# An instruction planner with other costs, gathered rows' readers placed later, and sums of squares on TensorE

## The chip, the cores and the metric

The kernel runs on one core of a Trainium2 chip. The metric is device time in microseconds (us) of one execution. The core has five engines that run their own instruction streams in order: PE (TensorE; its weight loads are listed as PEld), DVE (VectorE), ACT (ScalarE), POOL (GpSimd) and SP (SyncE, which here only starts DMA transfers).

## The reference, cut to what matters

One inference step of a two-layer decoder: 512 prompt tokens and 8 sample tokens (one new token for each of 8 sequences) with shared weights. Layer A is a Mamba-2 mixer (chunked scan, 4 groups, chunks of 128 tokens), layer B attention in three dilation groups against a shared K/V (for the sample rows: gathered from caches). Caches are also returned, shifted by one row.

```python
def mamba2_mixer(u, conv_prev, ssm_prev, w_in, conv_w, conv_b, dt_bias, a_log, d_skip, norm_w, w_out):
    z, xbc, dt = jnp.split(u @ w_in, [D_INNER, D_INNER + CONV_DIM], axis=-1)
    xbc, conv_new = causal_dwconv(xbc, conv_prev, conv_w, conv_b)
    ...
    y, ssm_new = ssd_scan(xs, dt, a, bm, cm, ssm_prev)      # h_t = exp(a*dt_t) h_{t-1} + dt_t x_t B_t^T, y_t = C_t h_t
    y = y + xs * d_skip[:, None]
    h = y * jax.nn.silu(z)
    hg = h.reshape(h.shape[:-1] + (SSM_GROUPS, D_INNER // SSM_GROUPS))
    hg = hg * lax.rsqrt(jnp.mean(hg * hg, -1, keepdims=True) + RMS_EPS)      # the sums of squares
    return (hg.reshape(h.shape) * norm_w) @ w_out, conv_new, ssm_new

def dilated_group_sample(q, k_all, v_all, buf_len, window, dil, slopes):     # 16 heads, 3 dilation groups
    steps = jnp.arange(window // dil + 1)
    idx = buf_len + jnp.arange(n_new)[:, None] - steps[None, :] * dil
    kg, vg = k_all[:, idx_c], v_all[:, idx_c]                                # gathered keys and values
    scores = jnp.einsum('bthd,btkhd->bthk', q, kg) * ATT_SCALE + bias
    ...
hp = layer_norm(DEEPNORM_ALPHA * hp + dp, ln_g[layer], ln_b[layer])          # after each layer
```

## The kernel before, in words

**A planner writes the order.** The kernel is built by Python generators on a clock of their own (class Order). Each generator issues instructions through an Eng object, which adds an estimated duration (Eng.cost) to that engine's planned time, and then sleeps until the planned end plus LAT (300 ns) before it issues what depends on it. What is emitted is one fixed instruction stream for each engine, in planned order; on the chip an engine takes its stream strictly in that order, and waits at the first instruction whose inputs are not there. A transfer's planned end comes from class Dma: a rate of 355 GB/s, some fixed delays, one queue. A Flag holds a tile's planned time; wait(flag) sleeps until then; take and give hand out the buffers of a pool; calm(engine) sleeps until the engine's planned queue is nearly empty; tt picks DVE or POOL, whichever is planned to end first. All instructions go through one helper line (157), so the profile's groups differ by tile names and not by lines; DMA issues have line 206.

**Layer A.** For each of four groups g the weights of x, B, C (6 tiles of 128 output columns) and later of the gate z (4 tiles) are loaded (`wst`), split into a rounded part and a rest (`whi` by ACT, `wlo` by DVE), and multiplied with the split input (tiles `xh`, `xl`): 48 matmuls a tile. The order is x0, x1, z0, x2, z1, x3, z2, z3. When the six x tiles of a group are planned, ssd(g) starts: for each chunk c of four, decay (M, CE from rows `Abc` read back by DMA), stage1 (CBm, xdt, xde), states (hst), stage2 (by, yt, the gate, and the sum of squares for the group's norm in v[:, 0, c]), and once a group sample(): eight sequences' states `hs` are loaded, multiplied with B and C rows (`bcb`), updated and stored. sample_end normalises the sample rows, and the group's own norm follows (tile hreg). Then the out projection out_unit runs over the groups (half 0: groups 0 to 3 with the split tiles hh, hl and for samples hsm; then half 1), the layer norm, and the split of its result (x1h, x1l).

**Layer B.** For each head pair hp of eight, ten projections (three K, V, Q and a gate; 48 matmuls each) alternate with attn(hp) for the prompt (scores from KT and QT tiles in 64 rows, P, then PT) and sample(hp) for the 8 samples. sample(hp) writes its query rows to DRAM (q_scr) and reads them back spread over all partitions: six loads `qb` through three buffers (qload). kgather loads three tiles `kg` of gathered keys a head pair, through two buffers. On DVE (or POOL) each half of a kg tile is multiplied with its qb and summed (tile sc); the scores then go through the softmax to the matmuls with `vg`. evac moves each projection out of PSUM: DVE writes the 8 sample columns (tile sT), ACT the rest (KT, QT, vT), and K and V tiles are transposed on PE. Between all of this the copier issues 168 pieces of the cache copy from ACT's queue. At the end the out projection of layer B and the layer norm run.

The lines the text speaks of: the costs in Eng.cost; stage2's sum of squares; one(), the per-sequence part of ssd's sample(); ssd's loop over chunks; kgather and qload. Their planned times of arrival are set so:

```python
f_kg[hp, g].t = end + LAT                       # kgather
f.t = dma(SP, qb, ...) + LAT                    # qload
yield from wait(fq); yield from calm(V, G)      # sample(hp)
end = tt(kt[:, bs], kt[:, bs], fq.tile, OP.mult)
```

Of the kernel before, what the change touches and what calls it, by code (L numbers as in the profile page):

```python
# [10 lines left out]
F32 = mybir.dt.float32  # L11
# [3 lines left out]
OP = mybir.AluOpType  # L15
AX = mybir.AxisListType

P = 128
# [16 lines left out]
RS = 2.0 ** -13  # L35
SLOPES = [2.0 ** (-8.0 * (h + 1) / 16) for h in range(16)]
LAT = 300.0
DMA_RATE = 355.0
ACT_ISSUE = 200.0
SMALL = 110.0  # L40
# [16 lines left out]
class Order:  # L57
# [8 lines left out]
    def spawn(self, gen, prio=1):  # L66
        self.seq += 1
        heapq.heappush(self.heap, (self.now, prio, self.seq, gen))
# [12 lines left out]
    def wait(self, *flags):  # L81
        for f in flags:
            while f.t is None:
                yield self.now + 100.0
            if f.t > self.now:
                yield f.t
# [41 lines left out]
class Eng:  # L128
    def __init__(self, order, raw, kind, port=None):
        self.o, self.raw, self.kind, self.free, self.port = order, raw, kind, 0.0, port  # L130

    def spend(self, cost, shared=False):
        t = max(self.free, self.o.now)
# [26 lines left out]
    def cost(self, name, a, k):  # L160
        if self.kind == "PE":
            mv = k["rhs"] if name == "matmul" else a[0]
            n = _n(mv)
            if name == "transpose":
                return 112.0
            if mv.dtype == F32:
                m = a[0].shape[0]
                return max(214.0, 4 * n / 2.4 + 4) * (0.35 if m == 32 else 0.63 if m == 64 else 1.0)
            return max(57.0, n / 2.4 + 13)
        if self.kind == "V":  # L170
            src = a[1]
            n = max(_n(a[0]), _n(src))
            if name in ("tensor_copy", "tensor_scalar") and not _psum(src):
                n /= 2
            if name == "reciprocal":
                n *= 6
            return (66 + n) / 0.96 + (SMALL if n < 64 else 15.0)
        if self.kind == "S":
            p = sum(1 for v in ("bias", "scale") if hasattr(k.get(v), "shape")) + (1 if "accum_out" in k else 0)
            return (112 + _n(a[0])) / 1.2 + 93 * p + 10  # L180
        n = _n(a[0])
        if name == "tensor_scalar":
            return 90 + 1.2 * n
        if name == "partition_broadcast":
            return 200 + 1.15 * n
        return 90 + (2.08 if name == "tensor_tensor" else 1.4) * n
# [27 lines left out]
def yoco_step(  # L214
# [17 lines left out]
    def dram(ap, off, dims):  # L232
        return bass.AP(tensor=ap.tensor, offset=ap.offset + off, ap=[list(d) for d in dims])
# [41 lines left out]
    def tt(out, a, b, op, slack=-100.0):  # L275

        n = _n(out)
        two = _sbuf(a) and _sbuf(b)
        ev = max(V.free, od.now, port.free if two else 0.0) + (66 + n) / 0.96
        eg = max(G.free, od.now, port.free) + 90 + 2.08 * n  # L280
        e = V if ev <= eg - slack else G
        e.tensor_tensor(out, a, b, op)
        return e.free
# [147 lines left out]
    def calm(*engines):  # L431

        while True:
            t = min(e.free for e in engines) - CALM
            if t <= od.now:
                return
            yield t
# [258 lines left out]

    f_hk = {(g, k): Flag() for g in range(GROUPS) for k in range(4)}
    f_hn = [Flag() for _ in range(GROUPS)]
    f_p = [Flag() for _ in range(GROUPS)]
    f_old = {(g, b): Flag() for g in range(GROUPS) for b in range(NS)}  # L700

# [10 lines left out]
    def ssd(g):  # L712
# [14 lines left out]
        def sample():  # L727
# [29 lines left out]
            def one(b, hs, end, bc):  # L757
                yield end + LAT
                tmp = yield from take(pN, [P, 4, P], "tmp", 2)
                yield from calm(V)  # L760
                for i in range(4):
                    V.tensor_tensor_reduce(tmp[:, i, :], hs[:, i, :], bc[:, 1, b % 2, :], 1.0, 0.0, OP.mult, OP.add, ys[:, i, b:b + 1])
                done[0] += 1
                if done[0] == NS:
                    f_s.t = V.free + LAT
                yield V.free + LAT
                yield from calm(S)
                for i in range(4):
                    S.activation(tmp[:, i, :], bc[:, 0, b % 2, :], AF.Copy, scale=xdts[:, i, b:b + 1])
                left[b // 2] += 1  # L770
                if left[b // 2] == 2:
                    give(pN, "bcb", S.free)
                yield S.free + LAT
                yield from calm(V)
                for i in range(4):
                    V.scalar_tensor_tensor(hs[:, i, :], hs[:, i, :], selv[:, 4 * g + i, b:b + 1], tmp[:, i, :], OP.mult, OP.add)
                give(pN, "tmp", V.free)
                yield V.free + LAT
                yield from dma.ready()
                give(pN, "hs", dma(S, dram(ssm_s, (b * DI + g * 512) * P, [[P, P], [P * P, 4], [1, P]]), hs))  # L780
                last[0] += 1
                if last[0] == NS:
                    give(pN, "xdts", S.free)
# [99 lines left out]
        def stage2(c):  # L883
# [32 lines left out]
            sq = yield from take(pS, [P, 4, P], "sq", 2)  # L916
            S.activation(sq, hv, AF.Square)
            yield S.free + LAT
            yield tt(sq[:, 0:2], sq[:, 0:2], sq[:, 2:4], OP.add, SLACK2) + LAT
            yield tt(sq[:, 0], sq[:, 0], sq[:, 1], OP.add, SLACK2) + LAT  # L920
            b = yield from bank()
            PE.matmul(b[:, 0:1], lhsT=sq[:, 0, :], rhs=ones[:, 0:1], start=True, stop=True)
            give(pS, "sq", PE.free)
            yield PE.free + LAT
            V.tensor_scalar(v[:, 0, c:c + 1], b[:, 0:1], 512.0 * EPS, None, OP.add)
            unbank(V.free)
            f_q[c].t = V.free

        def sample_end():
            yield from wait(f_s, f_sx, *[f_z[g, i] for i in range(4)])  # L930
# [28 lines left out]
            V.tensor_tensor(hv, hv, nw[:, 4 * g:4 * g + 4].unsqueeze(2).to_broadcast([P, 4, NS]), OP.mult)  # L959
            f_hn[g].t = V.free + LAT  # L960

        for c in range(4):
            for hg in range(2):
                spawn(decay(c, hg))
            spawn(stage1(c))
            spawn(states(c))
            spawn(stage2(c))
            if c == 0:
                spawn(sample())
            yield from wait(f_1[c])  # L970
        yield from wait(f_st[3])
        b = yield from bank()
# [376 lines left out]
    def layer_b(XB, pL, early):  # L1349
# [69 lines left out]
        def kgather():  # L1419
            for hp in range(8):  # L1420
                for g, (c, L, dil) in enumerate(caches):
                    kt = yield from take(pQ, [P, NS, P], "kg", 2)
                    end = dma(SP, kt, dram(c, hp * P, [[dil * ROW, P], [L * ROW, NS], [1, P]]))
                    f_kg[hp, g].tile = kt
                    f_kg[hp, g].t = end + LAT

        def vgather():
            for hp in range(8):
# [244 lines left out]
        def qload(hp, ready):  # L1673

            yield ready
            for g in range(3):
                for hb in range(2):
                    qb = yield from take(pB, [P, 4, P], "qb", 3)
                    f = f_qb[hp, g, hb]
                    f.tile = qb  # L1680
                    f.t = dma(SP, qb, dram(q_scr[hp], (g * NS + 4 * hb) * P, [[0, P], [P, 4], [1, P]])) + LAT
                    yield od.now

        def sample(hp):
# [256 lines left out]
```

## Time and profile before

| | us |
|---|---|
| median of 3 runs | 1242.2 |
| lowest and highest of them | 1235.66 and 1245.82 |
| the profiled execution | 1242.98 |
| its span, first to last instruction | 1241.2 |

The median is what a change is compared with. The profiled execution is the one that the trace shows; 1.8 us of it lie outside its span. Times in the rows below are us from the start of the span. An arrow in square brackets names the idle time of the engine just before an instruction and what ended it.

### The profile page before, as it was taken

Reading aid. Unit: us, or ns where it says so; the run is one execution under the profiler, and the core shown is the slowest. Engines: PE = TensorE matmul, PEld = TensorE weight load, DVE = VectorE, ACT = ScalarE, POOL = GpSimd, SP = SyncE. Lnnn points to the kernel's source line nnn. Section 1 sums busy time; section 2 is a strip of 40 time slices with the busy share of each in tenths; the row PEclk is TensorE's granted clock in tenths of the full one; section 3 lists DMA queues with packets and bytes.
Section 4 is the critical chain, followed back from the end, with each engine's and each line's share of the span. In section 5 each row is a group of like instructions: output and inputs, shape, how many; then the busy total and the mean of one; then the engine's idle time right before and its main releaser. Section 6 shows DMA issues by size and latency. Waiting matters only on the chain.

```text
span 1241.2 us, 23709 instructions
## 1 busy us (share of the span) xinstructions
PE 1124.5 (91%) x9114; PEld 1025.5 (83%) x9114; DVE 810.5 (65%) x2458; ACT 562.2 (45%) x1295; POOL 78.2 (6%) x152
## 2 busy tenths in 40 slices
PE   7999879989999799897999997989999999899994
PEld 6898869879886566897899897978989989899763
DVE  3989799799799647534727536346256373482878
ACT  3467766666666322343344442433334334333432
POOL 0011011020011001000001000010001000100000
PEclk9999979989999999899899998998999999999997
DMA  9889989898987888998899997998999989964421
GB/s 293 292 264 295 315 254 321 260 312 289 319 309 263 305 302 259 315 312 276 267 322 311 317 347 234 345 289 258 311 305 344 313 289 328 326 184 142 143 107 69
DMA packets 259466, 344.56 MB, mean 278 GB/s; under 512 B 10513, under 2 KB 240633, under 8 KB 256629
## 3 DMA queue, kind: packets, MB, share of 16 engines
q10 hardware_dynamic: 45068, 197.51, 44.4%
q1 hardware_dynamic: 214286, 145.55, 41.1%
q8 instruction: 71, 1.16, 0.4%
q14 instruction: 41, 0.34, 0.1%
HBM read 319.36 MB, written 199.82 MB: 418 GB/s over the span
## 4 chain that ended last, share of the span: by engine, by line
PE 45%; DMA 24%; DVE 22%; ACT 4%; issue 3%; SPq 1%; ACTq 0%; POOL 0%; DVEq 0%; POOLq 0%
PE ps L157 45%; DMA qb<-q_scr 5%; DVE wlo L157 3%; DMA bcb<-bc_scr 3%; DVE rt L157 3%; DMA wst<-in_a_in_proj_dram 2%; DMA wst<-in_kv_proj_dram 2%; DVE hreg L157 2%; DMA kg<-in_cache_kv_w_dram 2%; DMA out_dram<-hs 2%; DMA q_scr<-sq 2%; DMA Abc<-a_scr 2%; DVE xs L157 1%; ACT whi L157 1%; DVE al L157 1%
## 5 line engine op out<-in xcount | busy, mean ns | idle before, releaser
L157 PE MATMUL ps<-x1h,whi 128*128 128x256 f32 (+1 forms) x1280 | 281.8, 299 | 11.3 <-DVE G L157 11.3
L157 PE MATMUL ps<-x1l,whi 128*128 128x256 f32 (+1 forms) x1280 | 266.8, 287 | 0.0
L157 PE MATMUL ps<-x1h,wlo 128*128 128x256 f32 (+1 forms) x1280 | 266.7, 287 | 0.0
L157 ACT CAST whi<-wst 128x1024 fp32r<-128x1024 f32 x145 | 150.4, 1041 | 206.9 <-PE ps L157 177.8
L157 DVE TENSOR_TENSOR wlo<-wst,whi 128x1024 fp32r<-128x1024 f32 x143 | 174.3, 1222 | 96.2 <-ACT whi L157 88.0
L157 PEld LDWEIGHTS ps<-x1h,whi 128*128 128x128 f32 x1280 | 205.4, 195 | 18.8 <-DVE G L157 11.7
L157 PEld LDWEIGHTS ps<-x1l,whi 128*128 128x128 f32 x1280 | 205.7, 193 | 0.0
L157 PEld LDWEIGHTS ps<-x1h,wlo 128*128 128x128 f32 x1280 | 205.4, 193 | 0.0
L157 PE MATMUL ps<-xh,whi 128*128 128x256 f32 (+3 forms) x656 | 145.5, 299 | 3.4 <-DVE hreg L157 2.9
L157 PE MATMUL ps<-xl,whi 128*128 128x256 f32 (+3 forms) x656 | 135.4, 284 | 0.0
L157 PE MATMUL ps<-xh,wlo 128*128 128x256 f32 (+3 forms) x656 | 135.3, 284 | 0.0
L157 DVE TENSOR_SCALAR sT<-ps 128x8 f32<-128x8 f32 x72 | 11.8, 164 | 170.0 <-PE ps L157 169.9
L157 PEld LDWEIGHTS ps<-xh,whi 128*128 128x128 f32 (+1 forms) x656 | 103.3, 189 | 11.3 <-issue 6.1
L157 PEld LDWEIGHTS ps<-xl,whi 128*128 128x128 f32 (+1 forms) x656 | 102.9, 188 | 0.2
L157 PEld LDWEIGHTS ps<-xh,wlo 128*128 128x128 f32 (+1 forms) x656 | 102.6, 187 | 0.2
L157 ACT ACTIVATE P<-P,nm 128x256 f32<-128x256 f32 (+1 forms) x128 | 61.8, 486 | 51.1 <-DMA out_dram<-sq 12.6
L157 ACT COPY PT<-ps 128x512 f32<-128x512 f32 (+1 forms) x64 | 33.1, 564 | 61.0 <-PE ps L157 59.8
L157 DVE CUSTOM_DVE_ANT_0 P<-ps,bias 128x256 f32<-128x256 f32 (+1 forms) x128 | 46.7, 402 | 9.6 <-PE ps L157 8.6
L157 ACT ACTIVATE M<-Abc,ncs 128x128 f32<-128x128 f32 x128 | 40.8, 391 | 25.7 <-DMA Abc<-a_scr 17.2
L157 ACT ACTIVATE tmp<-bcb,xdts 128x128 f32<-128x128 f32 x128 | 40.5, 391 | 22.9 <-DVE ys L157 21.9
L157 POOL TENSOR_TENSOR kg<-kg,qb 128x512 f32<-128x512 f32 x8 | 10.4, 1303 | 607.8 <-DMA qb<-q_scr 272.1
L157 PE MATMUL ps<-whi,hh 128*128 128x512 f32 x120 | 48.4, 404 | 0.0
(282 smaller groups left out, 1862.4 us busy)
## 6 DMA issues: line engine op xcount, KB each, us to landing
wst<-in_kv_proj_dram SPq DMA_DIRECT2D x48, 512.0 KB
out_dram<-in_cache_kv_w_dram ACTq DMA_DIRECT2D x24, 1016.0 KB
wst<-in_a_in_proj_dram SPq DMA_DIRECT2D x16, 1024.0 KB
wst<-in_b_in_proj_dram SPq DMA_DIRECT2D x32, 512.0 KB
kg<-in_cache_kv_w_dram SPq DMA_DIRECT2D x24, 512.0 KB
vg<-in_cache_kv_w_dram SPq DMA_DIRECT2D x24, 512.0 KB
qb<-q_scr SPq DMA_DIRECT2D x48, 256.0 KB
hs<-in_state_ssm_dram SPq DMA_DIRECT2D x32, 256.0 KB
```

Of the source, the lines that this page charges most:

```text
L157: return raw(*a, **k)
```

## The change

Seven edits; the computation stays the same, and one step of it moves to another engine.

1. Gathered keys (kgather) and query rows (qload) are given a planned arrival 3500 ns later (LAZY). The transfers are the same.
2. Eng.cost for PE: a matmul in 4-byte floats costs at least 142 instead of 214 ns, and 0.28 or 0.51 of it in tiles of 32 or 64 (scores with 64 contraction rows now among them), with 115 ns for a turn between tiled and whole; a projection's matmul costs 2 ns less, a transpose 2 ns less.
3. Eng.cost for DVE: the 15 ns added to every instruction of 64 or more elements are dropped, and 45 ns are added to those with a scalar from a tile.
4. The sum of squares of a chunk: two additions (256 and 128 elements a partition) are dropped, and one matmul with a column of ones becomes four that accumulate.
5. In one(), the three calm() waits are dropped.
6. ssd(g) for g of 1 to 3 starts its chunks when the last sum of squares of group g-1 has been planned (f_seq).
7. ssd's sample() starts before that wait, at once when the group's x tiles are there.

```diff
@@ -35,6 +35,7 @@
 RS = 2.0 ** -13
 SLOPES = [2.0 ** (-8.0 * (h + 1) / 16) for h in range(16)]
 LAT = 300.0
+LAZY = 3500.0
 DMA_RATE = 355.0
 ACT_ISSUE = 200.0
 SMALL = 110.0
@@ -128,6 +129,7 @@
 class Eng:
     def __init__(self, order, raw, kind, port=None):
         self.o, self.raw, self.kind, self.free, self.port = order, raw, kind, 0.0, port
+        self.tiled = False
 
     def spend(self, cost, shared=False):
         t = max(self.free, self.o.now)
@@ -162,11 +164,15 @@
             mv = k["rhs"] if name == "matmul" else a[0]
             n = _n(mv)
             if name == "transpose":
-                return 112.0
+                return 110.0
+            m = a[0].shape[0]
+            tiled = mv.dtype == F32 and (m in (32, 64) or mv.shape[0] == 64)
+            turn = 115.0 if tiled != self.tiled else 0.0
+            self.tiled = tiled
             if mv.dtype == F32:
-                m = a[0].shape[0]
-                return max(214.0, 4 * n / 2.4 + 4) * (0.35 if m == 32 else 0.63 if m == 64 else 1.0)
-            return max(57.0, n / 2.4 + 13)
+                full = max(142.0, 4 * n / 2.4 + 6)
+                return turn + full * (0.28 if m == 32 else 0.51 if tiled else 1.0)
+            return turn + max(57.0, n / 2.4 + 11)
         if self.kind == "V":
             src = a[1]
             n = max(_n(a[0]), _n(src))
@@ -174,7 +180,8 @@
                 n /= 2
             if name == "reciprocal":
                 n *= 6
-            return (66 + n) / 0.96 + (SMALL if n < 64 else 15.0)
+            ptr = any(hasattr(v, "shape") for v in a[2:3]) and name in ("tensor_scalar", "scalar_tensor_tensor")
+            return (66 + n) / 0.96 + (SMALL if n < 64 else 45.0 if ptr else 0.0)
         if self.kind == "S":
             p = sum(1 for v in ("bias", "scale") if hasattr(k.get(v), "shape")) + (1 if "accum_out" in k else 0)
             return (112 + _n(a[0])) / 1.2 + 93 * p + 10
@@ -696,6 +703,7 @@
 
     f_hk = {(g, k): Flag() for g in range(GROUPS) for k in range(4)}
     f_hn = [Flag() for _ in range(GROUPS)]
+    f_seq = [Flag() for _ in range(GROUPS)]
     f_p = [Flag() for _ in range(GROUPS)]
     f_old = {(g, b): Flag() for g in range(GROUPS) for b in range(NS)}
 
@@ -757,21 +765,18 @@
             def one(b, hs, end, bc):
                 yield end + LAT
                 tmp = yield from take(pN, [P, 4, P], "tmp", 2)
-                yield from calm(V)
                 for i in range(4):
                     V.tensor_tensor_reduce(tmp[:, i, :], hs[:, i, :], bc[:, 1, b % 2, :], 1.0, 0.0, OP.mult, OP.add, ys[:, i, b:b + 1])
                 done[0] += 1
                 if done[0] == NS:
                     f_s.t = V.free + LAT
                 yield V.free + LAT
-                yield from calm(S)
                 for i in range(4):
                     S.activation(tmp[:, i, :], bc[:, 0, b % 2, :], AF.Copy, scale=xdts[:, i, b:b + 1])
                 left[b // 2] += 1
                 if left[b // 2] == 2:
                     give(pN, "bcb", S.free)
                 yield S.free + LAT
-                yield from calm(V)
                 for i in range(4):
                     V.scalar_tensor_tensor(hs[:, i, :], hs[:, i, :], selv[:, 4 * g + i, b:b + 1], tmp[:, i, :], OP.mult, OP.add)
                 give(pN, "tmp", V.free)
@@ -916,15 +921,16 @@
             sq = yield from take(pS, [P, 4, P], "sq", 2)
             S.activation(sq, hv, AF.Square)
             yield S.free + LAT
-            yield tt(sq[:, 0:2], sq[:, 0:2], sq[:, 2:4], OP.add, SLACK2) + LAT
-            yield tt(sq[:, 0], sq[:, 0], sq[:, 1], OP.add, SLACK2) + LAT
             b = yield from bank()
-            PE.matmul(b[:, 0:1], lhsT=sq[:, 0, :], rhs=ones[:, 0:1], start=True, stop=True)
+            for i in range(4):
+                PE.matmul(b[:, 0:1], lhsT=sq[:, i, :], rhs=ones[:, 0:1], start=i == 0, stop=i == 3)
             give(pS, "sq", PE.free)
             yield PE.free + LAT
             V.tensor_scalar(v[:, 0, c:c + 1], b[:, 0:1], 512.0 * EPS, None, OP.add)
             unbank(V.free)
             f_q[c].t = V.free
+            if c == 3:
+                f_seq[g].t = od.now
 
         def sample_end():
             yield from wait(f_s, f_sx, *[f_z[g, i] for i in range(4)])
@@ -959,14 +965,15 @@
             V.tensor_tensor(hv, hv, nw[:, 4 * g:4 * g + 4].unsqueeze(2).to_broadcast([P, 4, NS]), OP.mult)
             f_hn[g].t = V.free + LAT
 
+        spawn(sample())
+        if g:
+            yield from wait(f_seq[g - 1])
         for c in range(4):
             for hg in range(2):
                 spawn(decay(c, hg))
             spawn(stage1(c))
             spawn(states(c))
             spawn(stage2(c))
-            if c == 0:
-                spawn(sample())
             yield from wait(f_1[c])
         yield from wait(f_st[3])
         b = yield from bank()
@@ -1422,7 +1429,7 @@
                     kt = yield from take(pQ, [P, NS, P], "kg", 2)
                     end = dma(SP, kt, dram(c, hp * P, [[dil * ROW, P], [L * ROW, NS], [1, P]]))
                     f_kg[hp, g].tile = kt
-                    f_kg[hp, g].t = end + LAT
+                    f_kg[hp, g].t = end + LAT + LAZY
 
         def vgather():
             for hp in range(8):
@@ -1678,7 +1685,7 @@
                     qb = yield from take(pB, [P, 4, P], "qb", 3)
                     f = f_qb[hp, g, hb]
                     f.tile = qb
-                    f.t = dma(SP, qb, dram(q_scr[hp], (g * NS + 4 * hb) * P, [[0, P], [P, 4], [1, P]])) + LAT
+                    f.t = dma(SP, qb, dram(q_scr[hp], (g * NS + 4 * hb) * P, [[0, P], [P, 4], [1, P]])) + LAT + LAZY
                     yield od.now
 
         def sample(hp):
```

## Rows read from the trace of the kernel before

**Rows 1.** Busy time, share of the span, instructions of each engine (the page).

```profile
PE 1124.5 (91%) x9114; PEld 1025.5 (83%) x9114; DVE 810.5 (65%) x2458; ACT 562.2 (45%) x1295; POOL 78.2 (6%) x152
```

**Rows 2.** Two head pairs' stretches: length, busy (count) by engine, PEclk, DMA share, GB/s.

```profile
655.00:733.00 78.00, 75.34 (x696) 71.74 (x696) 43.61 (x147) 32.99 (x82) 3.69 (x4) 1.00 1.00 328
...
908.00:988.00 80.00, 77.26 (x704) 73.97 (x703) 43.17 (x146) 32.76 (x82) 3.54 (x4) 0.98 1.01 328
```

**Rows 3.** Timeline of PE: start, length, instruction, [idle before <-releaser], layer B's stalls.

```profile
592.66 0.48 PE L157 MATMUL ps<-ident,KT 128*128 128x128 f32 x1 [11.06 <-ACT KT L157]
...
671.57 0.33 PE L157 MATMUL ps<-ident,KT 128*128 128x128 f32 x1 [1.61 <-ACT KT L157]
...
755.33 0.48 PE L157 MATMUL ps<-ident,KT 128*128 128x128 f32 x1 [6.62 <-ACT KT L157]
...
861.75 0.28 PE L157 MATMUL ps<-ident,sc 128*16 128x128 f32 x1 [2.40 <-DVE sc L157]
...
926.35 0.33 PE L157 MATMUL ps<-ident,KT 128*128 128x128 f32 x1 [2.74 <-ACT KT L157]
...
1006.18 0.48 PE L157 MATMUL ps<-ident,KT 128*128 128x128 f32 x1 [2.69 <-ACT KT L157]
```

**Rows 4.** Timeline of DVE, ahead of the first of those stalls.

```profile
584.20 0.69 DVE L157 TENSOR_TENSOR kg<-kg,qb 128x512 f32<-128x512 f32 x1 [8.53 <-DMA qb<-q_scr]
...
592.04 0.15 DVE L157 TENSOR_SCALAR sT<-ps 128x8 f32<-128x8 f32 x1
```

**Rows 5.** Timeline of ACT, at the same stall.

```profile
592.23 0.38 ACT L157 ACTIVATE KT<-ps 128x256 f32<-128x256 f32 x1 [12.38 <-DVE sT L157]
```

**Rows 6.** Waits: who <- for what: us in total, times, longest.

```profile
DVE kg L157 <- DMA qb<-q_scr: 18.4, 6, 8.5
...
PE ps L157 <- DVE G L157: 12.4, 3, 6.0
```

**Rows 7.** Stretches with a lowered clock; columns as in rows 2.

```profile
861.00:870.00 9.00, 7.71 (x46) 6.27 (x47) 5.75 (x20) 3.81 (x13) 0.00 (x0) 0.62 0.90 260
...
926.00:931.00 5.00, 4.65 (x26) 4.65 (x27) 4.66 (x25) 0.91 (x4) 0.00 (x0) 0.66 0.79 262
...
157.00:184.00 27.00, 19.46 (x138) 15.25 (x139) 24.95 (x83) 14.87 (x38) 4.94 (x9) 0.75 0.76 239
...
256.00:272.00 16.00, 12.28 (x79) 9.70 (x78) 15.15 (x59) 11.28 (x28) 5.54 (x8) 0.68 1.09 359
```

**Rows 8.** Timeline of PE: the out projection waits for the last samples.

```profile
430.55 0.35 PE L157 MATMUL ps<-ones,sq 128*8 128x1 f32 x8 [4.03 <-ACT sq L157]
...
434.43 0.56 PE L157 MATMUL ps<-dgs,ones 8*128 8x8 f32 x2 [3.53 <-DVE dgs L157]
...
436.14 0.62 PE L157 MATMUL ps<-whi,hsm 128*40 128x512 f32 x1 [1.15 <-DVE hsm L157]
```

**Rows 9.** DVE groups by shape: count | busy us, mean ns | idle us.

```profile
L157 DVE TENSOR_TENSOR sq<-sq 128x256 f32<-128x256 f32 x13 | 6.2, 492 | 0.0
...
L157 DVE TENSOR_TENSOR sq<-sq 128x128 f32<-128x128 f32 x10 | 2.7, 279 | 0.0
```

**Rows 10.** Timeline of PEld: the weight loads of a sum of squares, the next.

```profile
166.82 0.30 PEld L157 LDWEIGHTS ps<-ones,sq 128*128 128x128 f32 x2
167.04 0.30 PEld L157 LDWEIGHTS ps<-xh,whi 128*128 128x128 f32 x2
```

**Rows 11.** Timeline of PE: group 3's first chunk; group 2's last sums.

```profile
308.36 0.27 PE L157 MATMUL ps<-ident,Bt 128*128 128x128 f32 x1
...
357.08 0.61 PE L157 MATMUL ps<-ones,sq 128*128 128x1 f32 x4
```

**Rows 12.** Timeline of PE: sixteen score matmuls of layer B.

```profile
566.69 1.16 PE L157 MATMUL ps<-KT,QT 64*128 64x128 f32 x16
```

**Rows 13.** Timeline of PE: its last wait for head pair 7's samples.

```profile
1195.71 0.50 PE L157 MATMUL ps<-whi,ol 128*128 128x512 f32 x1 [1.03 <-DVE ol L157]
```

**Rows 14.** Waits of SP's queue; columns as in rows 6.

```profile
SPq L206 <- DVE sc L157: 49.2, 14, 6.5
```

## The prediction

> **What bounds the kernel now.** I read the page first: TensorE (PE) is busy 1124.5 of 1241.2 us [rows 1]. So at most about 117 us can be had without taking work from PE, and the question is which of its pauses the change touches. Next I cut layer B into head pairs. The quickest takes 78 us, of which PE works 75.34; in that stretch, and in one of 80 us, the DMA engines' share is 1.00 and 1.01 [rows 2]. PE and the transfers are thus nearly in balance there, and other head pairs are longer because PE stops.
>
> Then PE's timeline: six stops of layer B end at a transpose that waits for a KT tile, or for the scores sc, together 11.06 + 1.61 + 6.62 + 2.40 + 2.74 + 2.69 = 27.1 us [rows 3]. The first, followed back: ACT's copy of KT waited 12.38 us for VectorE's (DVE's) little copy sT [rows 5]; sT, at 592.04, stood in DVE's stream behind the product kg x qb, at which DVE had waited 8.53 us for the transfer of qb [rows 4]. So a side chain (gathered keys of the samples) stops the main one because its reader was placed too early in an in-order stream. Waits of this kind on DVE add up to 18.4 us in six [rows 6]. After such a stop PE also runs slowly: behind the stops that ended at 861.75 and 926.35 the granted clock is 0.62 and 0.66 on average, so part of each stretch is at the lower of its two levels, 1.2 instead of 2.4 GHz [rows 7].
>
> In layer A DVE is the tight engine in places: in two stretches it is busy 24.95 of 27 and 15.15 of 16 us, PE only 19.46 and 12.28, at a clock of 0.75 and 0.68 [rows 7]. At the end of the first half of the out projection PE waits three times for the last group's sample rows, 4.03 + 3.53 + 1.15 = 8.7 us [rows 8].
>
> **The change part by part.** The sum is made against the profiled execution, 1243.0 us (its span and 1.8 outside).
>
> *Readers of kg and qb placed 3.5 us later.* Nothing is removed: for each head pair three kg loads, six qb loads, six products and six sums stay. The products come later in DVE's or POOL's stream, and what DVE has ready (the al copies, wlo, sT) moves ahead. Each stop shrinks by at most 3.5 us: 3.5 + 1.61 + 3.5 + 2.40 + 2.74 + 2.69 = 16.4 us [rows 3]. Bounds: nothing, if the transfer is late by as much again; 27.1, if sT itself gets ahead of the product. I take 16.4, as other engines' order shifts too. Two slow-clock stretches go with their stops: 9 x 0.38 + 5 x 0.34 = 5.1 us [rows 7]; bounds 0 and 5.1.
>
> *What the later readers hold up.* A kg or qb buffer is given back later, so the next load is issued later on SP, and the weight loads (wst) queued behind it wait too. SP already waits 49.2 us in 14 times for sc, the last reader of a kg tile [rows 14]. PE has three waits of 12.4 us in all for the gate tile G, the stop that late weights end in [rows 6]. I take one more of these, 12.4 / 3 = 4.1 us; bounds 0 and 49 (a rival below).
>
> *The last head pair.* Nothing follows it to fill the gap: PE waits for its sample rows as its last stop in layer B, 1.03 us [rows 13]. A third kg load issued later moves that chain by up to 3.5 us, all of it on PE: +3.5; bounds 0 and 7 (both flags in series).
>
> *Costs in the planner.* No instruction changes, only the order. Example: eight score matmuls (two records each) take 1.16 us [rows 12]; the old cost gives 8 x 217 = 1.74 us, the new one 8 x 112 + 115 = 1.01. With 24 such matmuls a head pair the plan had PE some 2.7 us later than it is. A DMA's reader was therefore set against too little PE work; this works in the same direction as the 3.5 us. I book it at nothing by itself.
>
> *Sums of squares.* 16 chunks lose two additions each: 23 on DVE, 6.2 + 2.7 = 8.9 us [rows 9], and 9 on POOL. PE gets 48 more matmuls of two records. Two loads for such a matmul take 0.22 us to the start of the next (166.82 to 167.04) [rows 10]: 48 x 0.22 = 10.6 us. Where PE waits for DVE the extra matmuls are hidden and the additions count; elsewhere the reverse. The stretches that DVE fills cover two of four groups: half of each, +5.3 - 4.5 = +0.8 us. Bounds -8.9 and +10.6.
>
> The trace has 0.11 us for each weight load here [rows 10]; the planner's new cost allows 142 ns for the whole matmul. The Trainium skill (TensorE: Matmul & The Clock Gate, LDWEIGHTS) has a load take the number of columns divided by 1.2 ns, 107 ns for 128, however little is streamed through. By that rule the 48 matmuls are 48 x 0.213 = 10.2 us, by the planner's constant 6.8; the rows agree with the page, and the plan will be some 3.5 us short on PE in layer A.
>
> *Sampled rows not held back, chunks held.* one() drops three calm waits, 128 products, 128 scalings and 128 updates move up in DVE's and ACT's streams; the chunks of groups 1 to 3 (with their 24 Abc loads on SP) wait in the plan for the sums of the group before. I expect the last group's sample rows to be ready when PE needs them: -8.7 us [rows 8]; bounds 0 and 8.7. What the held chunks gain or lose is unknown: a gain of up to the two stretches (27 - 19.46 + 16 - 12.28 = 11.3 us idle, 27 x 0.25 + 16 x 0.32 = 11.9 us of clock, 23 in all [rows 7]), a loss as below. I book nothing and keep both as rivals.
>
> Sum: 1243.0 - 16.4 - 5.1 + 4.1 + 3.5 + 0.8 - 8.7 = 1221.2 us. The profiled execution is 0.8 above the median of 1242.2, so the forecast is 1220 us.
>
> **The rivals.** (1) *Layer A's crowded stretches go too*: with group g's chunks behind group g-1's sums, DVE is never asked for both. For it: PE waits there on DVE alone. 1220 - 23 = 1197 us.
>
> (2) *The transfers take the gain*: where PE runs without stops the DMA share is already 1.00 and 1.01 [rows 2], so in shorter head pairs kg and qb land later still and the 3.5 us are eaten. Against it: after the last weights the engines have room, and the planner can leave copies until then. 1220 + 16.4 + 5.1 = 1242 us. The Trainium skill (DMA: Bandwidth & Descriptors, Issuing engines are not separate DMA queues) says that transfers from ACT and SP run on the same 16 engines and interleave. By that rule the cache copies delay the gathers whatever queue they are on; this is the same rival.
>
> (3) *The hold exposes the last group*: its first chunk is at 308.36, the last sums of group 2 at 357.08 [rows 11], 48.7 us between them. If ssd(3) starts that much later and half of it shows where PE needs group 3, and the sample gain is hidden behind it: 1220 + 24.4 + 8.7 = 1253 us, slower than before. It decides from some 13 us of delay. Against it: z2 is done earlier if PE has fewer chunks in between.
>
> (4) *SP's queue holds the weights*: 14 waits, each 3.5 us longer, each in front of a weight load that PE needs: 1220 + 49 = 1269 us. It outweighs the rest from about seven of the 14. Against it: a wst buffer is usually loaded a unit ahead.
>
> **How the numbers follow.** About 1% (12.4 us) is what a measurement of this kernel can tell from no change: faster is below 1229.8, slower above 1254.6. Forecast 0.46 (own range 1208 to 1233: the gathers between a half and all, the squares' bounds halved), rival 1 0.16, rival 2 0.17, rival 3 0.11, rival 4 0.10. Faster: 0.40 of the forecast, 0.16 and 0.02 of rival 2, 0.58. Slower: rival 4 and half of rival 3, 0.15. Same: 0.27. The range 1196 to 1255 leaves out rival 4, some of rival 3 and half of rival 1, together about 0.2.
>
> **What would show it.** Right: DVE's waits at kg fall well below 18.4 us, KT stops to about 11 us, sc sums after sT; no wait of PE for sq of samples ahead of the second half; PEld on sums of squares about 10 us more. Wrong: PE's waits for G above 20 us with SP waiting on sc far over 49 us (rival 4); PE waiting for hreg or hh of group 3 (rival 3); DMA share at 1.00 throughout layer B with DVE's waits at kg unchanged (rival 2).

## The result and the profile after

The changed kernel takes 1210.8 us (median of 4 runs, 1207.8 to 1211.5), the kernel before on the same chip 1244.0 (4 runs, 1235.7 to 1247.8). The ratio is 0.9737, with a 95% interval of 0.9683 to 0.9791. The forecast was 1220 us. The profiled execution took 1207.75 us, with a span of 1206.0. Of all executions below one, the 1214.8 us of e3, counts as slow: medians and ranges have it, ratios and intervals leave it out.

The page of the changed kernel, busy time, answering [rows 1]:

```profile
PE 1124.5 (93%) x9210; PEld 1028.7 (85%) x9210; DVE 806.4 (67%) x2443; ACT 561.6 (47%) x1295; POOL 65.2 (5%) x135
```

PE does 96 records more in the same busy time, so all of the 35.2 us of span came out of its idle time. (Its mean granted clock is 0.974 of full speed, 0.959 before.)

To see in which part, I cut the span at layer B's projections. Each kernel has one row for the 1280 matmuls `x1h,whi`, with the first and the last start. First the kernel before, then the changed one:

```profile
L157 PE MATMUL ps<-x1h,whi x1280: 276/283/583, 503.5 to 1157.6; 128*128 128x256 f32 x92, 128*128 128x264 f32 x91
```

```profile
L159 PE MATMUL ps<-x1h,whi x1280: 276/283/562, 494.7 to 1118.7; 128*128 128x256 f32 x92, 128*128 128x264 f32 x91
```

Up to the first one (called layer A below): 503.5 and 494.7, -8.8 us. From there to the last one (layer B): 654.1 and 624.0, -30.1. After it (the tail): 1241.2 - 1157.6 = 83.6 and 1206.0 - 1118.7 = 87.3, +3.7.

The whole of layer B, before and changed (columns as in [rows 2]):

```profile
503.50:1157.60 654.10, 612.73 (x5478) 585.82 (x5477) 329.26 (x1101) 257.18 (x635) 23.77 (x30) 0.96 0.91 291
```

```profile
494.70:1118.70 624.00, 606.72 (x5478) 579.52 (x5477) 328.52 (x1112) 258.75 (x640) 10.49 (x23) 0.99 0.95 308
```

On the same 5478 records PE's idle time falls from 41.4 to 17.3 us, by 24.1, and its busy time by 6.0, at a granted clock of 0.99 in place of 0.96.

PE's waits in the changed kernel (who <- for what: us in total, times, longest):

```profile
PE ps L159 <- ACT PT L159: 12.2, 5, 5.1
...
PE ps L159 <- DVE G L159: 5.4, 5, 2.1
...
PE ps L159 <- ACT hh L159: 2.0, 1, 2.0
PE ps L159 <- DVE hl L159: 1.9, 1, 1.9
...
PE ps L159 <- ACT KT L159: 0.6, 1, 0.6
```

The stops at KT and sc [rows 3] are gone but for 0.6 us, the waits for G fell from 12.4 [rows 6] to 5.4, and no wait for the samples' squares [rows 8] is left; `hh` and `hl`, which layer A's out projection reads, cost 2.0 and 1.9. PT, at which the kernel before had no stop, takes 12.2 us. Two stretches of head pairs (columns as in [rows 2]):

```profile
648.00:726.00 78.00, 76.06 (x701) 72.32 (x700) 40.18 (x129) 32.26 (x81) 1.35 (x3) 1.00 0.96 306
895.00:975.00 80.00, 77.58 (x702) 73.84 (x701) 42.30 (x147) 32.62 (x83) 1.26 (x3) 0.98 0.97 312
```

With PE nearly full, the DMA share is 0.96 and 0.97, below the 1.00 and 1.01 before; the transfers didn't take the gain back.

At the place of the first KT stop, DVE's timeline of the changed kernel reads:

```profile
572.52 0.16 DVE L159 TENSOR_SCALAR sT<-ps 128x8 f32<-128x8 f32 x1
572.60 1.22 DVE L159 TENSOR_TENSOR wlo<-wst,whi 128x1024 fp32r<-128x1024 f32 x1
573.73 0.68 DVE L159 TENSOR_TENSOR kg<-kg,qb 128x512 f32<-128x512 f32 x1
```

The small copy sT and the weight split wlo stand ahead of the first product kg x qb; before, sT stood behind it [rows 4]. But this order is not the whole account. The changed kernel without the shift (e2 below) has that product ahead of sT again, at 567.98 and 572.83, and still no PE stop at KT, while its layer B is as long as before. So the missing KT stops are not by themselves what the change gained.

### The profile page after: what moved, and what is told of

The parts are those of the page before. It is cut to its first block, busy times and chain, and to the rows that moved or that the text cites. A ratio compares the mean times of both kernels' runs of the same rounds, so it can differ in the third digit from the quotient of the medians.

```text
span 1206.0 us, 23879 instructions
## 1 busy us (share of the span) xinstructions
PE 1124.5 (93%) x9210; PEld 1028.7 (85%) x9210; DVE 806.4 (67%) x2443; ACT 561.6 (47%) x1295; POOL 65.2 (5%) x135
## 4 chain that ended last, share of the span: by engine, by line
PE 54%; DVE 18%; DMA 18%; ACT 6%; issue 2%; SPq 1%; ACTq 1%; DVEq 0%
PE ps L159 54%; DMA wst<-in_kv_proj_dram 6%; DVE wlo L159 3%; DMA Abc<-a_scr 3%; DVE rt L159 3%; DMA wst<-in_a_in_proj_dram 2%; DMA bcb<-bc_scr 2%; DMA qb<-q_scr 2%; ACT whi L159 1%; SPq L213 1%; DVE al L159 1%; DVE xs L159 1%; DVE lnmv L159 1%; ACT M L159 1%; DMA wst<-in_a_out_proj_dram 1%
## 5 line engine op out<-in xcount | busy, mean ns | idle before, releaser
L159 PE MATMUL ps<-x1h,whi 128*128 128x256 f32 (+1 forms) x1280 | 278.2, 295 | 4.5 <-DVE G L159 4.5
L159 PE MATMUL ps<-x1h,wlo 128*128 128x256 f32 (+1 forms) x1280 | 263.9, 285 | 0.0
L159 PE MATMUL ps<-x1l,whi 128*128 128x256 f32 (+1 forms) x1280 | 263.6, 284 | 0.0
L159 PEld LDWEIGHTS ps<-x1h,whi 128*128 128x128 f32 x1280 | 201.1, 191 | 13.4 <-DVE G L159 5.9
L159 PEld LDWEIGHTS ps<-x1h,wlo 128*128 128x128 f32 x1280 | 202.2, 190 | 0.0
L159 PEld LDWEIGHTS ps<-x1l,whi 128*128 128x128 f32 x1280 | 201.9, 190 | 0.0
L159 PEld LDWEIGHTS ps<-xh,whi 128*128 128x128 f32 (+1 forms) x656 | 103.0, 189 | 12.3 <-DVE hreg L159 5.2
L159 DVE TENSOR_SCALAR sT<-ps 128x8 f32<-128x8 f32 x72 | 11.8, 164 | 142.8 <-PE ps L159 142.5
L159 PE MATMUL ps<-ident,P 128*128 128x128 f32 x240 | 39.7, 284 | 12.2 <-ACT PT L159 12.2
L159 PE MATMUL ps<-whi,hl 128*128 128x512 f32 x120 | 48.1, 401 | 2.0 <-DVE hl L159 1.9
L159 ACT ACTIVATE M<-Abc,ncs 128x128 f32<-128x128 f32 x128 | 40.8, 391 | 18.8 <-DMA Abc<-a_scr 17.0
```

The lines of the kernel that those rows point to most:

```text
L159: return raw(*a, **k)
```

## The experiments

"The shift" is the 3.5 us (LAZY); "the layer A edits" are those to ssd (sums of squares, samples, hold); "the tables" are the durations in Eng.cost. One table for all runs; layer A, layer B and tail come from the profiled execution, cut as above. The kernel before took 1243.1 to 1244.0 us beside each of them.

| run | median us (range) | ratio, 95% interval | layer A | layer B | tail |
|---|---|---|---|---|---|
| before | 1242.2 (1235.7 to 1245.8) | | 503.5 | 654.1 | 83.6 |
| changed | 1210.8 (1207.8 to 1211.5) | 0.9683 to 0.9791 | 494.7 | 624.0 | 87.3 |
| e1_only_lazy | 1209.8 (1199.6 to 1215.4) | 0.9668 to 0.9804 | 501.0 | 613.3 | 88.9 |
| e2_after_without_lazy | 1232.0 (1225.0 to 1236.5) | 0.9875 to 0.9940 | 494.4 | 652.4 | 83.4 |
| e3_after_old_costs | 1199.9 (1196.6 to 1214.8) | 0.9606 to 0.9708 | 489.2 | 621.4 | 89.3 |
| e4_only_layer_a | 1232.2 (1225.3 to 1242.2) | 0.9892 to 0.9959 | 502.5 | 653.3 | 84.2 |
| e5_lazy_7us | 1204.5 (1201.9 to 1208.5) | 0.9645 to 0.9716 | 502.0 | 611.9 | 91.0 |
| e6_thin_copies | 1175.8 (1172.9 to 1176.5) | 0.9415 to 0.9471 | 480.7 | 607.6 | 86.1 |
| e7_old_pe_costs | 1218.4 (1216.7 to 1221.9) | 0.9756 to 0.9830 | 502.8 | 626.6 | 87.9 |
| e8_old_squares | 1223.1 (1211.3 to 1227.5) | 0.9755 to 0.9870 | 511.1 | 626.1 | 88.5 |
| e9_old_dve_costs | 1204.7 (1196.5 to 1207.7) | 0.9643 to 0.9748 | 495.9 | 620.9 | 89.2 |
| e10_no_hold | 1212.9 (1211.1 to 1218.4) | 0.9737 to 0.9823 | 501.2 | 620.1 | 88.1 |
| e11_no_hold_old_squares | 1207.3 (1201.6 to 1211.1) | 0.9665 to 0.9775 | 497.4 | 619.1 | 89.8 |
| e12_old_costs_lazy_7us | 1208.0 (1201.9 to 1213.5) | 0.9680 to 0.9783 | 499.2 | 616.2 | 92.7 |

One caution for reading it: kernels with the same order on PE up to layer B (before, e1, e5: 503.5, 501.0, 502.0; changed and e2: 494.7, 494.4; e3, e4, e12: 489.2, 502.5, 499.2) differ by up to 13 us in layer A (e4's profiled execution was the longest of its ten, 1242.2 us). A difference of that size there is not resolved by one profile, and with four runs each, medians less than about 8 us apart mostly have overlapping intervals; some that are farther apart, up to 15.8 us (e8 and e11), still overlap a little. Layer B is far steadier: 652.4 to 654.1 in the three kernels with the full cache copies and no shift, 611.9 to 626.6 in all with the shift.

### The shift alone, and all but the shift

The theory: the shift does most, as PE's stops at KT go. The rivals: the transfers take it back, or the layer A edits and tables do most.

The kernel before with edit 1 alone, in kgather and likewise in qload:

```diff
-                    f_kg[hp, g].t = end + LAT
+                    f_kg[hp, g].t = end + LAT + LAZY
```

> The kernel before with edit 1 alone (readers of kg and qb placed 3.5 us later in the plan; same instructions). Theory 1, the placement closes layer B's stops: 1243 less 20 to 27, so 1216 to 1223 us, and PE's stops at KT and sc fall from 27.1 us to under 6. Theory 2, the costs of the planner close them and the 3.5 us alone do little: 1235 us or more. Theory 3, any new order of this plan moves the time by some 10 us either way and the edit has no part of its own: anything from 1230 to 1255, with stops at KT of 15 us or more.

The kernel before with these two lines takes 1209.8 us, 33.5 less: as much as the whole change, and below the 1216 to 1223 of theory 1. Layer B is 613.3 us against 654.1:

```profile
501.00:1114.30 613.30, 601.47 (x5478) 574.62 (x5477) 329.50 (x1104) 256.48 (x635) 16.80 (x28) 0.99 0.95 310
```

PE's idle time in it falls from 41.4 to 11.8 us, and its busy time on the same records by 11.3. The waits (columns as above), then DVE's and PE's timelines:

```profile
DVE kg L158 <- DMA qb<-q_scr: 33.4, 10, 5.4
...
PE ps L158 <- DVE P L158: 10.4, 8, 3.0
```

```profile
575.07 1.22 DVE L158 TENSOR_TENSOR wlo<-wst,whi 128x1024 fp32r<-128x1024 f32 x1
576.30 0.17 DVE L158 TENSOR_SCALAR sT<-ps 128x8 f32<-128x8 f32 x1
581.82 0.69 DVE L158 TENSOR_TENSOR kg<-kg,qb 128x512 f32<-128x512 f32 x1 [5.36 <-DMA qb<-q_scr]
...
587.28 2.10 DVE L158 TENSOR_SCALAR P<-P,ee 128x256 f32<-128x256 f32 x2
```

```profile
588.73 1.39 PE L158 MATMUL ps<-ident,P 128*128 128x128 f32 x4 [3.00 <-DVE P L158]
```

DVE waits for qb longer than before, 33.4 us against 18.4 [rows 6], and yet PE has no stop at KT: wlo and sT have gone out before the wait. What still stands behind it is the scaling of the softmax's P, for which PE stops 3.00 us; its stops at P are 10.4 us in eight, against 0.4 in the kernel before. A wait in an in-order stream costs what stands behind it, not its length.

The converse, the changed kernel with LAZY = 0:

> The changed kernel with edit 1 undone (LAZY 0), the six other edits kept. Theory 1: the stops come back, 1211 plus 15 to 27, so 1226 to 1238 us, DVE's waits at kg 15 us or more in all. Theory 2: 1211 to 1218 us, waits at kg under 10 us. Theory 3: no clear side.

1232.0 us, 21.3 more than the changed kernel, inside the 1226 to 1238 of theory 1, and layer B is 652.4 us again. But the stops that came back are not those at KT, of which there is none: PE stops 25.9 us at PT and 9.8 at P. The longest, with SP, ACT and PE each in its own timeline of this run:

```profile
826.23 5.92 SPq L213 DMA_DIRECT2D qb<-q_scr  x1
```

```profile
835.40 0.63 ACTq L213 DMA_DIRECT2D out_dram<-tokK  x1
836.07 0.59 ACT L159 COPY PT<-ps 128x512 f32<-128x512 f32 x1 [9.40 <-DMA wst<-in_kv_proj_dram]
```

```profile
836.71 0.48 PE L159 MATMUL ps<-ident,P 128*128 128x128 f32 x1 [7.57 <-ACT PT L159]
```

ACT starts transfers from its own stream. Its copy of PT stood behind the issue of the tokK store, which went out at 835.40 after SP had spent 5.92 us on issuing one qb load. In the changed kernel the four longest stops at PT, 11.8 of the 12.2 us, stand behind a store of tokK or tokV in the same way; the longest, in PE's and ACT's timelines:

```profile
1062.34 0.48 PE L159 MATMUL ps<-ident,P 128*128 128x128 f32 x1 [5.14 <-ACT PT L159]
```

```profile
1061.03 0.63 ACTq L213 DMA_DIRECT2D out_dram<-tokV  x1
1061.70 1.07 ACT L159 COPY PT<-ps 128x512 f32<-128x512 f32 x2 [6.55 <-DMA wst<-in_kv_proj_dram]
```

What the store's issue waited for, no row shows; the transfers that the rows name as releasers belong to SP's queue. So the shift's worth, 21.3 us, is measured here too, but its way only in part. The stops at P go from 9.8 us to nothing; the longest, 3.17 us, stands behind a wait of DVE of 5.32 us for a kg tile. Why later readers cut the stops at PT from 25.9 to 12.2 us, no run shows.

### Is 3.5 us enough, and what makes the loads late

The same kernel, the one before with the shift alone, with twice the shift:

```diff
-LAZY = 3500.0
+LAZY = 7000.0
```

> The kernel before with the readers of kg and qb placed 7 instead of 3.5 us later. Theory 1a, what counts is that sT and wlo stand ahead of the first product in DVE's stream: the 3.5 us have already done that, so the same time as with edit 1 alone, 1203 to 1216 us, though DVE's waits at kg fall from 33 us (with 3.5 us) to under 10. Theory 1b, DVE's waiting time itself costs: as the waits fall by 20 us or more, the time falls by 5 us or more again, to 1205 us or less. Theory 1c, buffers held longer push the later loads out: 1220 us or more, SP waiting longer for sc.

1204.5 us, 5.2 below the 3.5 us version, with overlapping intervals. The time lies in the ranges of both 1a and 1b, so it doesn't tell them apart; layer B does:

```profile
502.00:1113.90 611.90, 600.01 (x5477) 574.35 (x5476) 324.96 (x1108) 257.02 (x635) 10.50 (x24) 0.99 0.94 311
```

DVE's waits for qb fall from 33.4 us to 5.8, and layer B only from 613.3 to 611.9: removing 27 us of DVE's waits bought 1.4. PE's idle time in it is 11.9 us, as with 3.5 us (11.8): its stops at P fall from 10.4 to 2.4 us, and others come, at PT 6.0 and at vT 3.2. The tail grows from 88.9 to 91.0.

Next, the kernel before with each cache copy moving an eighth of its bytes (7/8 of the returned caches are not written; the plan still counts them whole, so the order is unchanged):

```diff
-            dma(S, dram(o, oo, [[m // 16, 16], [1, m // 16]]), dram(c, co, [[m // 16, 16], [1, m // 16]]))
+            dma(S, dram(o, oo, [[m // 16, 16], [1, m // 128]]), dram(c, co, [[m // 16, 16], [1, m // 128]]), 8)
```

> The kernel before, order of all instructions unchanged, but each piece of the cache copy moves an eighth of its bytes (the copied rows of the cache outputs are mostly left out), the plan counting the whole. Theory C, the copies make the gathers late: DVE's waits at kg fall from 27.5 us (qb and kg) to under 8, PE's stops at KT from 24.7 to under 5, and the time to 1195 to 1220 us, the two waits for G included. Rival D, the way from q_scr to qb (write, wait, read) is late by itself: stops at KT stay at 15 us or more and the time above 1228 us.

1175.8 us with no shift at all, below the 1195 to 1220 of theory C: layer A, where no gathered row is read, is 22.8 us shorter too (480.7 against 503.5). The waits:

```profile
DVE kg L157 <- DMA kg<-in_cache_kv_w_dram: 2.1, 4, 0.7
...
PE ps L157 <- ACT KT L157: 1.7, 1, 1.7
...
DVE kg L157 <- DMA qb<-q_scr: 0.6, 1, 0.6
```

PE's stops at KT fell from 24.7 us [rows 3] to 1.7, DVE's waits for qb from 18.4 [rows 6] to 0.6. Rival D had 15 us or more at KT. So it is the copies, which ACT starts, that make SP's gathers late. This is rival 2's premise, and it is true; its conclusion, that the transfers take the gain, is not. The Trainium skill (DMA: Bandwidth & Descriptors, Issuing engines are not separate DMA queues) says that transfers of both issuers interleave on the same 16 engines; this run agrees.

### The layer A edits alone

Edits 4 to 7 of the change put on the kernel before: sums of squares on PE, three calm waits dropped, chunks held, samples first; no shift, old tables.

> The kernel before with edits 4 to 7 alone (sums of squares on TensorE, sample rows not held back, chunks held), layer B's code and the costs as before. Theory 1: layer A gives some 8 to 12 us and layer B nothing, 1231 to 1236 us; the first half of layer A's out projection no longer waits 8.7 us for samples; stops at KT about 27 us as before. Theory 3: layer B's stops differ by 10 us or more although nothing of it was touched.

1232.2 us, 11.0 less than the 1243.3 of the kernel before beside it. Layer B stays at 653.3, though its stops are not the same: 16.7 us at KT, where about 27 were expected, and 14.7 at G. Where in layer A the 11.0 us lie, this run can't show: the profiled execution was the longest of the ten, and its layer A is 1.0 us shorter than before. Alone, the shift gives 33.5 and these edits 11.0; 1243.3 - 33.5 - 11.0 = 1198.8 is, within the spread of the runs, what the two together, with the old tables, came to in the next run (1199.9).

### The tables

The changed kernel with all old durations, with only PE's old, and with only DVE's old (the diff is DVE's part; PE's is taken back in the same way):

```diff
-            ptr = any(hasattr(v, "shape") for v in a[2:3]) and name in ("tensor_scalar", "scalar_tensor_tensor")
-            return (66 + n) / 0.96 + (SMALL if n < 64 else 45.0 if ptr else 0.0)
+            return (66 + n) / 0.96 + (SMALL if n < 64 else 15.0)
```

> The changed kernel with edits 2 and 3 undone (the planner's old costs for PE and DVE), edits 1 and 4 to 7 kept. Theory 1: 1211 to 1218 us, stops at KT under 6 us. Theory 2: 1225 us or more, because the plan again has PE some 2.7 us too late in every head pair.

> The changed kernel with edit 2 alone undone (old costs for PE, new for DVE). With both old costs it ran 1200 instead of 1211 us, so the new costs lose 11. If the PE costs lose it (PE planned faster, so that transposes of P are reached before ACT's copies): 1198 to 1204 us, PE's waits for PT under 4 us instead of 12. If the DVE costs lose it: 1208 to 1215 us, waits for PT as they were.

> The changed kernel with the old VectorE durations (edit 3 undone) and the new TensorE ones. It completes the four pairs of duration tables: both new 1211, only VectorE's new 1218, both old 1200. Theory that VectorE's new durations lose and TensorE's gain or change nothing: 1192 to 1203 us. Rival, that each order is a throw of its own and the tables have no price apart: 1205 to 1222 us.

| | DVE new | DVE old |
|---|---|---|
| PE new | 1210.8 (changed) | 1204.7 (e9) |
| PE old | 1218.4 (e7) | 1199.9 (e3) |

No instruction differs, only the order. Against what I had expected of e3 (1211 to 1218), the old tables are quicker. DVE's new durations cost 6.1 and 18.5 us in the two comparisons; the second pair has intervals apart, the first not. PE's give 7.6 and cost 4.8, no verdict. Of the other two expectations, e7's 1218.4 fits neither side, nor do its waits for PT (5.3 us, for under 4 or some 12), and e9's 1204.7 falls between the two that I had set for it. In layer B the four differ by 5.7 us at most (620.9 to 626.6). Why DVE's new durations lose isn't settled: that a plan without spare time in it puts readers too early would fit, but no run tells this from chance in the order. e3 has the lowest median of the versions with the whole output, 0.9% below the changed kernel; the two intervals overlap (0.9606 to 0.9708, 0.9683 to 0.9791).

### The squares and the hold

All four with the old tables and the shift. Squares on VectorE again:

```diff
-            for i in range(4):
-                PE.matmul(b[:, 0:1], lhsT=sq[:, i, :], rhs=ones[:, 0:1], start=i == 0, stop=i == 3)
+            yield tt(sq[:, 0:2], sq[:, 0:2], sq[:, 2:4], OP.add, SLACK2) + LAT
+            yield tt(sq[:, 0], sq[:, 0], sq[:, 1], OP.add, SLACK2) + LAT
+            PE.matmul(b[:, 0:1], lhsT=sq[:, 0, :], rhs=ones[:, 0:1], start=True, stop=True)
```

> The changed kernel with both old costs (1200 us) and with edit 4 undone as well: sums of squares again with two additions and one matmul. By the prediction's term (0.8 us, bounds -8.9 and +10.6) no difference, 1196 to 1204 us. If the additions on DVE count: 1206 us or more. If the extra matmuls on PE count: 1194 us or less.

and the hold removed, with either kind of squares:

```diff
-        if g:
-            yield from wait(f_seq[g - 1])
```

> The changed kernel with the old durations of both engines and without the hold of the chunks (edit 6 undone); sums of squares on TensorE, samples first. With the hold and all else equal it took 1200. Theory, that the hold costs nothing as long as the sums are early: 1196 to 1204 us. Rival, that the hold itself costs some us also with early sums: 1185 to 1195 us.

> As the run without the hold, and with the sums of squares on VectorE as before the change. With the hold this took 1223. Theory, that the sums of squares cost only through the hold, which makes the next group's chunks wait for late sums: within 5 us of the run without the hold, 1196 to 1206 us. Rival, that sums on TensorE give their 20 us whatever holds the chunks: 1215 to 1226 us.

| | squares on PE | squares on VectorE |
|---|---|---|
| hold | 1199.9 (e3) | 1223.1 (e8) |
| no hold | 1212.9 (e10) | 1207.3 (e11) |

With the hold the squares on PE are worth 23.2 us, without it they cost 5.6 (not resolved). The theory that old squares cost only through the hold stands, if barely by its own numbers (e11 is 1207.3 for 1196 to 1206, and 5.6 from e10): the rival's 1215 to 1226 is missed by 7.7. The intervals of e8 and e11 overlap a little (0.9755 to 0.9870, 0.9665 to 0.9775); their stops at the sums, below, differ in the same sense. But the hold is not neutral, as that theory had it for e10 (1196 to 1204; the rival had 1185 to 1195): both missed. PE's waits at the sums, e8 and then e11:

```profile
PE ps L158 <- DVE sq L158: 8.4, 3, 4.1
```

```profile
PE ps L158 <- DVE sq L158: 1.1, 1, 1.1
```

and the stretches of layer A, e3 and then e8 (columns as in [rows 2]):

```profile
110.00:240.00 130.00, 122.89 (x1056) 116.43 (x1056) 118.33 (x378) 83.32 (x201) 12.76 (x18) 0.97 0.95 310
240.00:340.00 100.00, 94.77 (x786) 88.43 (x785) 92.24 (x298) 67.21 (x159) 5.11 (x10) 0.97 0.89 289
```

```profile
110.00:240.00 130.00, 119.88 (x999) 112.19 (x998) 116.31 (x364) 80.10 (x192) 7.45 (x14) 0.95 0.90 298
240.00:340.00 100.00, 88.33 (x719) 82.52 (x717) 88.59 (x290) 61.89 (x150) 10.55 (x17) 0.93 0.91 300
```

With the hold, the next group's chunks stand behind a chain, in e8 through two VectorE additions; PE waits there, is 3.0 and 6.4 us less busy in the two stretches, and its granted clock is 0.95 and 0.93 against 0.97. Whether the hold with early sums gains is open: e3 against e10 says 13.0 us, but e12, which has e3's order in layer A, ran on e10's chip at 1208.0, 4.9 less.

### The best of both

The changed kernel with the old tables and LAZY = 7000:

> The changed kernel with the old durations of both engines and a shift of 7.0 us in place of 3.5. With 3.5 it took 1200. On the kernel before 7.0 against 3.5 gave 1204.5 against 1209.8. If what is left of that gain stands beside the layer A edits: 1192 to 1198 us. If 3.5 us already took all there is: 1198 to 1204 us.

1208.0 us, above both expectations (1192 to 1198, 1198 to 1204), and not better than e3. Layer B is 5.2 us shorter than e3's, the tail 3.4 longer, and layer A, in the same order, 10.0 longer in the profiled executions.

## Why the prediction came out right, and which terms were wrong

*What bounds the kernel*: right in the main. Gathered rows' readers placed too early in DVE's stream stopped PE; with the shift alone the KT stops go and layer B loses 40.8 us (e1). The KT stops were too narrow a sign of it: e2 has none and an equally long layer B, with stops at PT and P.

*Readers of kg and qb later, -16.4, clock -5.1, late weights +4.1*: together -17.4, measured -30.1 in layer B, and -21.3 in the medians of e2 and the changed kernel. The clock was near: 6.0 us of the 30.1 are PE's busy time. The stops were not: PE's idle time fell by 24.1 us, for 16.4 - 4.1 = 12.3 booked. The mis-sized step is "each stop shrinks by at most 3.5 us". A shift is not subtracted from a stop: it changes which instruction stands first. Once sT and wlo are ahead of the product, PE's whole 11.06 us stop [rows 3] goes, though DVE still waits 5.36 us for qb; 3.00 us come back at P (e1). My own upper bound, 27.1, named that case ("if sT itself gets ahead of the product"); I should have taken it, since DVE had the al copies, wlo and sT to put there. The weights' +4.1 did not come: PE's waits for G fell from 12.4 to 5.4 us. The changed kernel also has 12.2 us of waits at PT, which I had not foreseen; how much of them is the shift's is open, since e2 has more.

*The last head pair, +3.5*: about right. The tail grew by 3.7 us, in the other kernels with 3.5 us by 4.3 to 6.2; with 7 us in e5 and e12 by 7.4 and 9.1. In the three kernels with the full cache copies and no shift it is 83.4 to 84.2.

*Tables, 0*: wrong. The example was right (PE's scores were costed too dear), the inference that truer durations do no harm was not. By the medians the kernel is some 11 us slower with them (e3; the intervals overlap a little). DVE's, which I had not costed at all, are the part that a run resolves: 18.5 us beside PE's old ones (e7 against e3); beside PE's new ones 6.1, not resolved (e9).

*Squares, +0.8*: wrong as a sum of its own. I costed engine time; the runs show a chain: 23.2 us gained with the hold, nothing resolved without. The engine time itself was near. PEld in the changed kernel:

```profile
146.29 0.98 PEld L159 LDWEIGHTS ps<-ones,sq 128*128 128x128 f32 x8
147.19 0.30 PEld L159 LDWEIGHTS ps<-xh,whi 128*128 128x128 f32 x2
```

A chunk's eight loads take 0.90 us to the start of the next, for 0.22 with two [rows 10]: 16 x 0.68 = 10.9 us more, for a forecast of 10.6.

*Samples, -8.7*: the waits at sq, dgs and hsm are gone, and layer A is 8.8 us shorter, close to -8.7 + 0.8. One profile of layer A is worth less than that looks (the caution above); all layer A edits together gave 11.0 us by medians (e4), and no run has the samples' edits by themselves.

*The rivals.* 1 (layer A's stretches go too, 1197): no, all of layer A is 8.8 us shorter, for the 8.7 of the samples and 23 more. 2 (the transfers take the gain): the loads are late because of the copies (e6), but a late load costs only what stands behind its reader: in e1 10.4 us at P, where layer B still lost 40.8. 3 (the hold exposes the last group): not in the changed kernel, where hh and hl cost 3.9 us; by the medians the hold cost 15.8 us where the sums were late (e8 against e11). 4 (SP's queue holds the weights): SP's waits for sc are 56.9 us in 15 against 49.2 in 14 [rows 14], and PE's waits for G fell.

*What would show it*: KT stops "about 11" were 0.6. "DVE's waits at kg fall well below 18.4" came true (7.4) and was the wrong sign to watch: in e1 they rose to 33.4, in e3 to 37.0, and both are at least as quick.

So the total came within 10 us although two terms were off by more: the gain in layer B was booked too small, and the loss by the tables not at all. That these two have opposite signs is luck.

## What to carry to other kernels

Where an engine's order is fixed beforehand, don't price a wait by its length but by what stands behind it: ask what moves ahead if the late reader moves back, and book the whole stop if that is what the next engine waits for. Then see what is left behind the reader, since the next stop will be there. A change that only alters a planner's estimates is not free; a truer cost table needs its own timing. Edits that share a chain (an addition, and a hold that waits for its result) must be priced together.

## What the runs showed of the hardware

A transfer's issue can itself take microseconds and hold up the engine that issues it. The row for the qb loads (issue time: min/median/max ns), before and with thin copies:

```profile
L206 SPq DMA_DIRECT2D qb<-q_scr x48: 319/339/4631, 573.5 to 1175.5; - x48
```

```profile
L206 SPq DMA_DIRECT2D qb<-q_scr x48: 319/338/1011, 545.1 to 1107.1; - x48
```

The longest takes 4.63 us with the full copies and 1.01 with an eighth of their bytes; in the changed kernel it is 6.15 us. In e2, SP's next issue starts at 832.25, when the 5.92 us of the one before are over. On ACT, which also copies out of PSUM for PE, the issues themselves are short (0.63 us for a store of tokK), but one that went out late held up the copy behind it, and PE stopped for 7.57 us (e2). And two executions with the same order on PE differed by 13 us by the end of layer A, so a single profile is no measure of a change of a per cent.
